# A decoder layer's conv norm: Newton product in the bank, later matmuls, longer VectorE estimates in the planner

## The chip, the cores and the metric

The kernel runs on one core of one Trainium2 chip. The metric is the time of the device for one execution in microseconds (us); the kernel is run several times and the median counts. The core has five engines with a queue each, worked off in order: TensorE (PE in the profile; PEld is its loading of weights), VectorE (DVE), ScalarE (ACT), GpSimd (POOL) and SyncE (SP), which issues the DMAs here. An engine waits at the head of its queue until what it needs is there, and everything behind that instruction waits with it.

## What is computed

One layer with two mixers side by side on 1024 positions of width 1024, in float32:

```python
def group_rms_norm(x, g, n_groups, eps=NORM_EPS):
    shp = x.shape
    xg = x.reshape(shp[:-1] + (n_groups, shp[-1] // n_groups)).astype(jnp.float32)
    y = xg * lax.rsqrt(jnp.mean(xg * xg, axis=-1, keepdims=True) + eps)
    return (y.reshape(shp) * g.astype(jnp.float32)).astype(x.dtype)

def hybrid_mixer(u, w_in, conv_w, conv_norm_g, ret_norm_g, w_out):
    z = u @ w_in
    ...
    y_conv = cb * causal_dwconv3(cc * ch, conv_w)
    y_conv = group_rms_norm(y_conv, conv_norm_g, CONV_GROUPS)
    ...
    y_ret = group_rms_norm(o, ret_norm_g, RET_HEADS) * jax.nn.silu(rg)
    return jnp.concatenate([y_conv, y_ret], axis=-1) @ w_out

h = h + hybrid_mixer(rms_norm(h, norm1_g), w_in, conv_w, conv_norm_g, ret_norm_g, w_out)
h = h + sq_relu_mlp(rms_norm(h, norm2_g), w_up, w_down)
return rms_norm(h, final_norm_g)
```

The part of interest is `y_conv`: 512 channels in 8 groups of 64, each group of each position divided by its root mean square.

## The kernel before

Everything lies transposed: channels on the 128 partitions, positions along the free axis in two halves of 512, so that a tile is 128 x 1024 and an instruction works on 128 x 512. A column tile of `z = u @ w_in` is 128 output channels. For each float32 product the two factors are split into a high part and a rest (`wh` and `wl` for weights, `uh` and `ul` or the two halves of `U` for the right-hand side), and three matmuls hi x hi, hi x lo and lo x hi stand for one; all are 128 x 128 by 128 x 512 into a bank of PSUM. The high part of a piece of weights is a cast on ScalarE, the rest (`wl<-r,wh`) a subtraction on VectorE or GpSimd (`split_piece`); both have four buffers.

The columns go by turns: retention's q and k first, then column tiles 0 to 3 and 20 whole (`whole`), then four pairs (4,5), (6,7), (8,9), (10,11) by `pair_in`, then 21 whole, and at the end 22 and 23. A pair is worked out with seven products of 12 matmuls in place of eight; it needs sums of weight blocks (`r<-r,r`, on GpSimd) and sums of the right-hand side (`xs`, `U`), and VectorE adds each product from its bank to the parts of the result (`z<-z,b`). The conv group i has the three tiles 3i (C), 3i+1 (h) and 3i+2 (B); tiles 20 to 23 are gates. What follows a tile are small programs written as generators: `conv_h` forms a = C * h * R2 and the three-tap convolution `cv` (ScalarE starts it, VectorE adds two taps: `cv<-z,sm,cv`), `conv_b` forms B * R * cv and asks for the norm, `gate` does SiLU, `split_y` splits y for the output product.

`norm` (from L468) serves one conv tile and half: ScalarE squares (`t`) and casts to the high part (`s<-t`), VectorE or GpSimd takes the rest (`s<-t,s`), two matmuls with a block matrix of ones, `blkr` (L483 and L484), add the squares over each group of 64 channels into a bank. Then ScalarE takes a reciprocal root `rt` and from it `less` = rt^2 / (2 x 64), and VectorE refines by one Newton step: `less` = (bank + 64 eps) * less, then in `done` (L712) y = y * (-g) * rt and y = (less - 1.5) * y. In the profile these three are `r<-b,r`, `z<-z,less_g,r` and `z<-r,z`.

The order in all queues is set when the program is built. A planner (`background`) keeps a clock for TensorE, `now`, moved on by 2.72 us for each product or quarter tile (`slot`), and a clock for each of the other three. A generator yields what it wants next: a tuple of engines (the planner gives it the one that would be done first, and goes on with the generator that is done first of all), a key that another one marks, or a number: the time that must have passed between its data being ready and `now` before its matmuls are put into TensorE's queue. A yield is thus a point at which another program's instruction may be put in between. `Engine.cost` is the estimate for one instruction: a fixed part and one per column; for VectorE, where no argument is in a bank, up to as much again while GpSimd's clock is ahead. The wrapper `Engine` records every instruction, so that the profile puts them all on L74. Weight pieces are split by `prepare` in a fixed order; there the choice between VectorE and GpSimd hangs on the two clocks, too.

Of the kernel before, what the change touches and what calls it, by code (L numbers as in the profile page):

```python
# [13 lines left out]
ALU = mybir.AluOpType  # L14
# [13 lines left out]
EPS = 1e-6  # L28
# [12 lines left out]
IN_END = [22, 23]  # L41
SLOT, LOOK, PE_MARGIN, LATE = 2.72, 3.2, 1.2, 0.0
WARM = 10
NORM_MARGIN, STEP_MARGIN = 4.0, 0.3
UP_ORDER, MLP_ORDER = (1, 2, 5, 6, 3, 7, 4), (1, 2, 6, 5, 3, 7, 4)


class Engine:
# [7 lines left out]
    def cost(self, n, op="", bank=False):  # L56
        per_column = 6.3 if op == "reciprocal" else self.per_column
        cost = self.fixed + 1e-3 * n * per_column
        if self.beside and not bank and op != "reciprocal":
            begin = max(self.clock[self], self.now[0])  # L60
            cost += min(cost, max(0.0, 0.6 * (self.clock[self.beside] - begin)))
        return cost

    def __getattr__(self, op):
# [15 lines left out]
def hybrid_layer(  # L80
# [21 lines left out]
    dve = Engine(nc.vector, 0.13, 1.04, now, clock, pool)  # L102
# [17 lines left out]
    def nm(s):  # L120
        n_[0] += 1
        return f"{s}{n_[0]}"
# [6 lines left out]
    def tmp():  # L129
        return temps[-1].tile([P, H], F32, tag="t", name=nm("t"))  # L130

    def bank(pool_=None):
        return (pool_ or pm).tile([P, H], F32, tag="b", name=nm("b"))

    def f32(ap):
        return ap.bitcast(F32)
# [106 lines left out]
    b = bank(pr)  # L243
# [181 lines left out]
    def mark(key, eng):  # L425
        got[key] = clock[eng]
# [44 lines left out]
    def norm(y, w, inv_n, done):  # L471

        sq = tmp()
        sh = xp.tile([P, H], F32R, tag="s", name=nm("s"), bufs=4)
        yield (act,)
        act.square(sq, y)
        act.copy(sh, sq)
        eng = yield (dve, pool)
        slo = xp.tile([P, H], F32R, tag="s", name=nm("s"), bufs=4)
        eng.tensor_sub(slo, sq, f32(sh))  # L480
        yield NORM_MARGIN
        b = bank(pr)
        nc.tensor.matmul(b, w, sh, start=True, stop=False)  # L483
        nc.tensor.matmul(b, w, slo, start=False, stop=True)  # L484
        now[0] += 0.43
        yield (act,)
        rt = xp.tile([P, H], F32, tag="s", name=nm("r"), bufs=4)
        less = xp.tile([P, H], F32, tag="s", name=nm("r"), bufs=4)
        act.activation(rt, b, AF.Abs_reciprocal_sqrt, bias=eps, scale=inv_n)
        act.activation(less, rt, AF.Square, scale=(0.5 * inv_n) ** 0.5)  # L490
        yield (dve,)

        dve.scalar_tensor_tensor(less, b, EPS / inv_n, less, ALU.add, ALU.mult)
        yield from done(rt, less)
        parts_of_s[0] -= 2

    def norms():
        while asked and parts_of_s[0] <= 2:
            parts_of_s[0] += 2
            y, w, inv_n, done, ready, late = asked.pop(0)  # L500
            spawn(norm(y, w, inv_n, done), ready, late)
# [200 lines left out]
    def conv_b(i, half, z, out, psum):  # L702
        sl = hs[half]
        o = out[:, sl]
        eng = dve if psum else (yield (pool, dve))
        eng.tensor_mul(o, z, R[:, sl])
        yield "cv", i, half
        eng = yield (pool, dve)
        eng.tensor_mul(o, o, cvs[i][:, sl])
        y[i] = out  # L710

        def done(rt, less):  # L712
            yield (dve,)
            dve.scalar_tensor_tensor(o, o, less_g[:, i : i + 1], rt, ALU.mult, ALU.mult)
            dve.scalar_tensor_tensor(o, less, 1.5, o, ALU.subtract, ALU.mult)
            mark(("y", i, half), dve)

        asked.append((o, blkr, 1.0 / 64, done, clock[eng], LATE * half))
# [531 lines left out]
    for at, (n, p) in enumerate((n, p) for n in MLP_ORDER for p in range(EARLY)):  # L1250
        b = early[p].product(n)
# [311 lines left out]
```

## Time and profile before

| | |
|---|---|
| median of 3 runs | 1080.27 us (1080.08 to 1080.79) |
| the profiled execution | 1081.81 us |
| its span, first to last instruction | 1079.0 us |
| granted TensorE clock, mean | 0.997 |
| PE busy | 1060.5 us (98%) |
| DVE busy | 878.7 us (81%) |
| POOL busy | 538.0 us (50%) |
| ACT busy | 460.2 us (43%) |

The profile is of one execution. A busy TensorE is not one at its full rate: matmuls overlap, and the starts of two that follow each other tell more than their durations. In the rows, `out<-in` gives the tiles by name, without their numbers; "idle before" is the time in which the engine stood still just before, and the arrow names what ended that.

### The profile page before, as it was taken

How to read it: one execution, taken by the hardware profiler on the slowest of the kernel's cores; microseconds unless marked ns; L12 is line 12 of the kernel's file. 1: busy time of each engine (PE TensorE's matmuls, PEld its weight loads, DVE VectorE, ACT ScalarE, POOL GpSimd, SP SyncE). 2: the span in 40 equal slices, each digit the busy share in tenths (PEclk: the TensorE clock that was granted, in tenths of full speed). 3: DMA queues.
4: the chain of work that ended last, by engine and by line, in shares of the span. 5: the costliest groups of instructions: out<-in, count | busy, mean ns of one | idle time of the engine just before them, and what ended most of it. 6: DMA issues, size and time to landing. Idle time of an engine off the chain costs nothing.

```text
span 1079.0 us, 13854 instructions
## 1 busy us (share of the span) xinstructions
PE 1060.5 (98%) x4860; PEld 881.6 (82%) x4860; DVE 878.7 (81%) x1246; ACT 460.2 (43%) x904; POOL 538.0 (50%) x366
## 2 busy tenths in 40 slices
PE   9999999999989999999999999999999999999997
PEld 7888888887768888788788888888888888888886
DVE  7446546799998656699999989989899899899955
ACT  8211445663435544444433443433343344334453
POOL 6234223255753223559538358267276185384552
PEclk9999999999999999999999999999999999999999
DMA  7111122222223635050121211201301301200204
GB/s 274 62 59 39 40 70 78 75 79 73 78 59 118 215 104 188 1 195 21 48 88 39 69 49 49 79 30 57 90 21 50 98 20 50 88 20 20 69 30 156
DMA packets 39685, 82.25 MB, mean 76 GB/s; under 512 B 4544, under 2 KB 5696, under 8 KB 39616
## 3 DMA queue, kind: packets, MB, share of 16 engines
q1 hardware_dynamic: 39328, 80.85, 23.0%
q8 instruction: 38, 0.62, 0.2%
q10 hardware_dynamic: 288, 0.52, 0.1%
q14 instruction: 31, 0.25, 0.1%
HBM read 71.92 MB, written 9.44 MB: 75 GB/s over the span
## 4 chain that ended last, share of the span: by engine, by line
PE 79%; DVE 10%; POOL 4%; issue 3%; ACT 2%; DMA 1%; DVEq 0%; SPq 0%; POOLq 0%; ACTq 0%
PE b L403 46%; PE b L1276 22%; PE b L357 4%; PE b L1385 4%; DVE wl L74 2%; DVE z L74 2%; POOL z L74 1%; POOL r L74 1%; DVE t L74 1%; DVE x L74 1%; DVE U L74 1%; DVE q L74 1%; DVE xs L74 1%; ACT h L74 1%; DVE m L74 1%
## 5 line engine op out<-in xcount | busy, mean ns | idle before, releaser
L403 PE MATMUL b<-U,wh 128*128 128x512 f32 x1024 | 315.8, 390 | 1.8 <-DVE x L74 1.1
L74 ACT CAST wh<-r 128x512 fp32r<-128x512 f32 x286 | 175.9, 620 | 321.2 <-PE b L403 134.5
L74 DVE TENSOR_TENSOR wl<-r,wh 128x512 fp32r<-128x512 f32 x251 | 231.8, 926 | 91.4 <-ACT wh L74 90.5
L74 POOL TENSOR_TENSOR r<-r,r 128x512 f32<-128x512 f32 x136 | 209.9, 1546 | 116.3 <-DVE wl L74 65.6
L1276 PE MATMUL b<-V,wh 128*128 128x512 f32 x784 | 242.0, 389 | 0.5 <-POOL V L74 0.4
L403 PEld LDWEIGHTS b<-U,wh 128*128 128x128 f32 x1024 | 191.8, 188 | 42.6 <-issue 1.9
L74 DVE TENSOR_TENSOR x<-x,b 128x512 f32<-128x512 f32 (+1 forms) x312 | 195.6, 673 | 30.2 <-PE b L1385 14.2
L403 PE MATMUL b<-U,wl 128*128 128x512 f32 x512 | 199.5, 390 | 0.3 <-POOL wl L74 0.3
L1276 PEld LDWEIGHTS b<-V,wh 128*128 128x128 f32 x784 | 147.1, 188 | 32.3 <-POOL V L74 0.8
L74 POOL TENSOR_TENSOR t<-t,t 128x512 f32<-128x512 f32 x70 | 106.4, 1524 | 97.9 <-ACT t L74 51.9
L1276 PE MATMUL b<-V,wl 128*128 128x512 f32 x392 | 152.5, 389 | 0.0
L74 POOL TENSOR_TENSOR wl<-r,wh 128x512 fp32r<-128x512 f32 x35 | 48.6, 1394 | 160.7 <-ACT wh L74 153.5
L403 PEld LDWEIGHTS b<-U,wl 128*128 128x128 f32 x512 | 96.2, 188 | 21.2 <-POOL wl L74 0.7
L403 PE MATMUL b<-uh,wh 128*128 128x512 f32 x304 | 103.4, 399 | 2.3 <-DVE z L74 2.3
L403 PE MATMUL b<-uh,wl 128*128 128x512 f32 x304 | 100.8, 391 | 1.1 <-DVE wl L74 1.1
L403 PE MATMUL b<-ul,wh 128*128 128x512 f32 x304 | 101.0, 392 | 0.0
L1276 PEld LDWEIGHTS b<-V,wl 128*128 128x128 f32 x392 | 73.5, 188 | 15.2
L74 POOL TENSOR_TENSOR V<-t,V 128x512 fp32r<-128x512 f32 x35 | 49.6, 1416 | 67.3 <-ACT V L74 67.3
L74 DVE TENSOR_TENSOR t<-t,b 128x512 f32<-128x512 f32 x112 | 75.8, 677 | 1.7 <-POOL t L74 1.2
L74 ACT ACTIVATE t<-t 128x512 f32<-128x512 f32 x64 | 40.2, 631 | 79.8 <-DVE t L74 79.2
L74 DVE TENSOR_TENSOR V<-t,V 128x512 fp32r<-128x512 f32 x63 | 70.3, 1116 | 0.0
L403 PEld LDWEIGHTS b<-uh,wl 128*128 128x128 f32 x304 | 57.3, 189 | 13.9 <-DVE wl L74 1.5
(178 smaller groups left out, 1422.1 us busy)
## 6 DMA issues: line engine op xcount, KB each, us to landing
r<-w_up_t SPq DMA_DIRECT2D x64, 256.0 KB, 2.6
r<-w_down_t SPq DMA_DIRECT2D x56, 256.0 KB, 2.7
r<-w_in_t SPq DMA_DIRECT2D x48, 256.0 KB, 2.7
xt<-xT SPq DMA_DIRECT2D x16, 256.0 KB, 5.4
xs<-xT SPq DMA_DIRECT2D x8, 512.0 KB, 4.9
r<-w_out_t SPq DMA_DIRECT2D x16, 256.0 KB, 2.7
x<-xT SPq DMA_DIRECT2D x8, 512.0 KB, 8.9
k<-x SPq DMA_DIRECT2D x6, 512.0 KB, 3.2
```

Of the source, the lines that this page charges most:

```text
L74: return f(out, *args, **kw)
L357: nc.tensor.matmul(vb[i], a[k][:, i * P : (i + 1) * P], b[k // 2][:, vs], start=(k == 0 and a is uh and b is vh), stop=(k == KT - 1 and a ...
L403: nc.tensor.matmul(b, a[:, k, :], rhs(n, k)[r], start=(start and i == 0), stop=(stop and i == len(ops) - 1),)
L1276: nc.tensor.matmul(b, a, r, start=(i == 0), stop=(i == len(ops) - 1))
L1385: nc.tensor.matmul(z, a, b, start=(k == 0 and t == 0), stop=(k == 3 and t == 2))
```

## The change

Three things are changed, and the planner then puts many instructions elsewhere.

- The planner: the wait in front of a norm's matmuls is 6.5 us in place of 4.0, and VectorE's estimate is lengthened as if GpSimd's clock stood 1.0 us later than it does.
- The first Newton product writes its result into the bank of the sums in place of the tile `less`. The last product reads it there, so that it has one input in PSUM and one in SBUF.
- A yield stands between the last two products.

```diff
-NORM_MARGIN, STEP_MARGIN = 4.0, 0.3
+NORM_MARGIN, STEP_MARGIN, POOL_LATE = 6.5, 0.3, 1.0
...
-            cost += min(cost, max(0.0, 0.6 * (self.clock[self.beside] - begin)))
+            cost += min(cost, max(0.0, 0.6 * (self.clock[self.beside] + POOL_LATE - begin)))
...
-        dve.scalar_tensor_tensor(less, b, EPS / inv_n, less, ALU.add, ALU.mult)
-        yield from done(rt, less)
+        dve.scalar_tensor_tensor(b, b, EPS / inv_n, less, ALU.add, ALU.mult)
+        yield from done(rt, b)
...
         def done(rt, less):
             yield (dve,)
             dve.scalar_tensor_tensor(o, o, less_g[:, i : i + 1], rt, ALU.mult, ALU.mult)
+            yield (dve,)
             dve.scalar_tensor_tensor(o, less, 1.5, o, ALU.subtract, ALU.mult)
             mark(("y", i, half), dve)
```

The number of instructions on TensorE is the same. VectorE's queue has 1170 rows where it had 1185, GpSimd's 384 where it had 370; in the stretch of the norms VectorE gives four net and GpSimd takes six more. Of the two orders below the numbers behind a name count tiles in the order of their making, so they differ from one program to the other; what tells the places apart are the names in front.

First piece: TensorE's queue, where before the norm of conv tile 2, first half, stood at the end of pair (8,9) (bank b_2683) and ahead of pair (10,11) (b_2717). Before:

```order
L403 MATMUL b_2683<-U_2224,wh_2602 128x512 x2
L403 MATMUL b_2683<-U_2224,wl_2603 128x512
L483 MATMUL b_2703<-s_2612,blkr 128x512
L484 MATMUL b_2703<-s_2634,blkr 128x512
L403 MATMUL b_2717<-uh_157,wh_2626 128x512
L403 MATMUL b_2717<-ul_165,wh_2626 128x512
```

Now the norm's bank is b_2747, and it stands behind the second product of pair (10,11), b_2727, ahead of the third, b_2758:

```order
L403 MATMUL b_2727<-uh_164,wh_2645 128x512
L403 MATMUL b_2727<-ul_172,wh_2645 128x512
L403 MATMUL b_2727<-uh_164,wl_2646 128x512
L483 MATMUL b_2747<-s_2631,blkr 128x512
L484 MATMUL b_2747<-s_2655,blkr 128x512
L403 MATMUL b_2758<-U_1566,wh_2670 128x512 x2
```

The norm's two matmuls moved by two products, 24 matmuls. The six norms of conv tiles 1 to 3 move by 12, 24, 24, 24, 12 and 24; the two of conv tile 0 by 12 each.

Second piece: VectorE's queue towards the end of pair (10,11): a norm's Newton products and the adding of products, down to the bank that column tile 21 takes over next (b_2813 before, b_2803 now). Before:

```order
L74 SCALAR_TENSOR_TENSOR cv_2759<-z_2536,sm,cv_2759 128x511
L74 SCALAR_TENSOR_TENSOR cv_2759<-z_2536,sm,cv_2759 128x510
L74 SCALAR_TENSOR_TENSOR r_2784<-b_2780,r_2784 128x512
L74 SCALAR_TENSOR_TENSOR z_2535<-z_2535,less_g,r_2783 128x512
L74 SCALAR_TENSOR_TENSOR z_2535<-r_2784,z_2535 128x512
L74 TENSOR_TENSOR z_2716<-z_2716,b_2792 128x512
L74 TENSOR_TENSOR z_2715<-z_2716,b_2761 128x512
L74 TENSOR_TENSOR z_2715<-z_2715,b_2813 128x512
```

Now:

```order
L74 SCALAR_TENSOR_TENSOR b_2747<-b_2747,r_2751 128x512
L74 SCALAR_TENSOR_TENSOR z_2535<-z_2535,less_g,r_2750 128x512
L74 TENSOR_TENSOR wl_2772<-r_2606,wh_2771 128x512
L74 SCALAR_TENSOR_TENSOR z_2535<-b_2747,z_2535 128x512
L74 SCALAR_TENSOR_TENSOR cv_2777<-z_2536,sm,cv_2777 128x511
L74 SCALAR_TENSOR_TENSOR cv_2777<-z_2536,sm,cv_2777 128x510
L74 TENSOR_TENSOR z_2702<-z_2702,b_2782 128x512
L74 TENSOR_TENSOR z_2701<-z_2702,b_2758 128x512
L74 TENSOR_TENSOR z_2701<-z_2701,b_2803 128x512
```

What stands ahead of the last three is the first half's Newton step where it was the second half's, with a low half of weights between its last two products. Further up, in pair (6,7), the low half of the fifth product stood behind two `cv` products (cv_2250 twice, then wl_2376) and now stands ahead of them (wl_2373, then cv_2269 twice).

Third piece: GpSimd's queue in pair (8,9): the sums of weight blocks for pair (10,11) (`r`), B * R of conv tile 2 (z_2535 with R) and low halves. Before:

```order
L74 TENSOR_TENSOR wl_2650<-r_2554,wh_2649 128x512
L74 TENSOR_TENSOR r_2578<-r_2578,r_2606 128x512
L74 TENSOR_TENSOR r_2529<-r_2578,r_2529 128x512
L74 TENSOR_TENSOR r_2554<-r_2554,r_2529 128x512
L74 TENSOR_TENSOR r_2578<-r_2606,r_2529 128x512
L74 TENSOR_TENSOR s_2710<-t_2659,s_2660 128x512
L74 TENSOR_TENSOR wl_2731<-r_2554,wh_2730 128x512
```

Now:

```order
L74 TENSOR_TENSOR z_2535<-z_2535,cv_2559 128x512
L74 TENSOR_TENSOR r_2579<-r_2579,r_2606 128x512
L74 TENSOR_TENSOR r_2522<-r_2579,r_2522 128x512
L74 TENSOR_TENSOR r_2554<-r_2554,r_2522 128x512
L74 TENSOR_TENSOR r_2579<-r_2606,r_2522 128x512
L74 TENSOR_TENSOR z_2535<-z_2535,R 128x512
L74 TENSOR_TENSOR wl_2717<-r_2554,wh_2716 128x512
```

A product with `cv`, which VectorE did before, now stands ahead of the four sums, and one with `R` ahead of the low half; a norm's rest (`s_2710`) has gone to VectorE.

## The prediction

> **What bounds the kernel now.** I read the table of stages first, then the waits of TensorE, then its timeline at each wait, and last the groups of VectorE and GpSimd in the same stretch. The table of stages (busy time and count of each engine, granted clock, DMA) shows a stretch in which TensorE runs without a break and the 100 us in which the conv norms are worked off:
>
> ```profile
> 360.00:380.00 20.00, 20.00 (x90) 16.58 (x89) 12.52 (x18) 10.10 (x18) 2.97 (x2) 1.00 0.72 255
> 240.00:340.00 100.00, 94.55 (x400) 75.35 (x399) 91.62 (x105) 44.00 (x73) 53.88 (x36) 0.98 0.28 90
> ```
>
> TensorE does 90 matmuls in 20 us where nothing holds it, and 400 in the 100 us from 240 to 340, 40 to 50 fewer than at that rate. VectorE is busy for 91.6 of those 100 us: here it is the engine that others wait for. Elsewhere the kernel is a nearly unbroken row of matmuls that the change leaves as they are. TensorE's own waits between 234 and 340 us (what ended them: total, times, longest):
>
> ```profile
> PE b L403 <- DVE z L74: 2.3, 1, 2.3
> PE b L403 <- DVE wl L74: 1.1, 1, 1.1
> PE b L483 <- ACT s L74: 1.0, 1, 1.0
> ```
>
> The ends of matmuls are modelled, so I price each wait from start to start in TensorE's timeline (start, duration, line, count, idle time before):
>
> ```profile
> 265.52 0.39 PE L403 MATMUL b<-ul,wh 128*128 128x512 f32 x1
> 267.03 0.50 PE L403 MATMUL b<-uh,wl 128*128 128x512 f32 x1 [1.12 <-DVE wl L74]
> 267.37 0.40 PE L403 MATMUL b<-uh,wh 128*128 128x512 f32 x1
> ...
> 269.70 0.47 PE L484 MATMUL b<-s,blkr 128*128 128x512 f32 x1
> 270.13 0.51 PE L483 MATMUL b<-s,blkr 128*128 128x512 f32 x1
> 270.86 0.50 PE L484 MATMUL b<-s,blkr 128*128 128x512 f32 x1 [0.22 <-DVE s L74]
> 271.20 0.62 PE L403 MATMUL b<-U,wh 128*128 128x512 f32 x2
> ...
> 295.80 0.40 PE L403 MATMUL b<-U,wl 128*128 128x512 f32 x1
> 297.17 0.50 PE L483 MATMUL b<-s,blkr 128*128 128x512 f32 x1 [0.97 <-ACT s L74]
> 297.89 0.50 PE L484 MATMUL b<-s,blkr 128*128 128x512 f32 x1 [0.23 <-DVE s L74]
> 298.23 0.40 PE L403 MATMUL b<-uh,wh 128*128 128x512 f32 x1
> ...
> 306.41 0.39 PE L483 MATMUL b<-s,blkr 128*128 128x512 f32 x1
> 307.13 0.50 PE L484 MATMUL b<-s,blkr 128*128 128x512 f32 x1 [0.33 <-DVE r L74]
> 307.46 0.62 PE L403 MATMUL b<-U,wh 128*128 128x512 f32 x2
> ...
> 317.68 0.62 PE L403 MATMUL b<-U,wh 128*128 128x512 f32 x2
> 318.14 0.39 PE L403 MATMUL b<-U,wl 128*128 128x512 f32 x1
> 318.36 0.39 PE L403 MATMUL b<-uh,wh 128*128 128x512 f32 x1
> 321.06 0.79 PE L403 MATMUL b<-uh,wh 128*128 128x512 f32 x1 [2.31 <-DVE z L74]
> ...
> 324.74 0.62 PE L403 MATMUL b<-uh,wl 128*128 128x512 f32 x2
> ```
>
> From 317.68 to 318.36 three matmuls start in 0.68 us, 0.227 each; what a step takes beyond that is lost. Four terms come out. **N**, the norms' own matmuls, whose input is not ready: 0.20 + 0.50 + 0.11 after 269.70, 1.14 + 0.49 + 0.11 after 295.80, 0.49 + 0.10 after 306.41, together 3.1 us. **W**, a weight piece's low half late at 267: 1.28 + 0.11 = 1.4 us. **B**, a bank that VectorE has not emptied at 321: 2.70 − 0.23 = 2.5 us. **C**, slow matmuls behind B: the nine that start from 321.06 to 324.74 take 3.68 us where 2.04 would do, 1.6 us. The sum is 8.6 us, and nothing in this stretch can bring more than that but for small change.
>
> **The change: the norms' matmuls.** The wait in front of them goes from 4.0 to 6.5 us of the planner's time, and its slot is 2.72, so they move by one product or two. The first piece of order shows one that stands 24 matmuls later, 5.4 us at 0.227; the two at 269 move by 12 and 24, the one at 306 by 24. None of the waits in N was over 1.8 us, so inputs that are ready when they were would no longer be waited for: N is worth up to 3.1. Behind a late norm wait its Newton products on VectorE and then y; the last y is needed by the output products, 72 matmuls (16 us) behind the last norm now, so I cost that delay at nothing; without that cover it would be up to 5.4. In the same place ScalarE gets two more table loads, since a gate now falls between the last two norms:
>
> ```profile
> 336.63 1.28 ACT L74 ACT_TABLE_LOAD x1
> ```
>
> 2 × 1.28 = 2.6 us under the same 16 us: nothing.
>
> **The change: VectorE and GpSimd.** What each instruction costs there, first the groups between 234 and 334 us (count, busy, mean ns), then all between 215 and 340 us (ns: least, median, most), and three in a row:
>
> ```profile
> L74 DVE TENSOR_TENSOR wl<-r,wh 128x512 fp32r<-128x512 f32 x17 | 19.7, 1158 | 3.2 <-ACT wh L74 3.0
> L74 DVE SCALAR_TENSOR_TENSOR z<-r,z 128x512 f32<-128x512 f32 x5 | 6.4, 1277 | 0.2
> L74 POOL TENSOR_TENSOR r<-r,r 128x512 f32<-128x512 f32 x12 | 17.9, 1496 | 4.0 <-DMA r<-w_in_t 2.3 <-DVE wl L74 1.3
> ```
> ```profile
> L74 DVE TENSOR_TENSOR wl<-r,wh x18: 675/692/1783, 221.7 to 333.8; 128x512 fp32r<-128x512 f32 x18
> L74 DVE SCALAR_TENSOR_TENSOR r<-b,r x8: 676/679/683, 228.7 to 337.6; 128x512 f32<-128x512 f32 x8
> L74 DVE SCALAR_TENSOR_TENSOR z<-r,z x8: 691/1177/1672, 230.5 to 339.0; 128x512 f32<-128x512 f32 x8
> ```
> ```profile
> 305.84 0.67 DVE L74 TENSOR_TENSOR z<-z,b 128x512 f32<-128x512 f32 x1
> 306.44 0.68 DVE L74 SCALAR_TENSOR_TENSOR r<-b,r 128x512 f32<-128x512 f32 x1
> 307.04 1.82 DVE L74 SCALAR_TENSOR_TENSOR z<-z,less_g,r 128x512 f32<-128x512 f32 x1
> ```
>
> An instruction with one input in a bank takes 0.68 always; one with both in SBUF takes 0.69 or anything up to 1.8. The difference is GpSimd: VectorE's 105 instructions at the step of 0.60 that the last three rows show would be 63 us, it was busy for 91.6, and the excess of 28.6 over GpSimd's 36 instructions is 0.8 us for each. One that GpSimd does costs it 1.50.
>
> Newton's last product now reads the bank, and a weight piece may go between the last two (second piece of order). From the evacuation of column tile 20 to the bank of B, VectorE has 80 instructions before and 75 now: 49 with both inputs in SBUF become 41 (four last products that now read a bank, four net that went elsewhere), 31 with a bank become 34. GpSimd has 33 in that part before, 39 now. The account at mean prices: four products from 1.28 to 0.68 save 2.4, four moved ones at 1.16 save 4.6, one more of 0.68 gone makes 7.7 us off VectorE; six more on GpSimd put back 0.8 each, 4.8. Net 2.9 us. The ends: 7.7 if none of the six meets VectorE, and with the removed ones at their price alone (0.69) 3.4 − 6 × 1.1 = −3.2, where 1.1 is 1.78 − 0.68.
>
> VectorE paces TensorE here, so this account and not the list of waits sets the sum. Up to the bank TensorE was 7.0 us behind an unbroken run (N 3.1, W 1.4, B 2.5). 7.0 − 2.9 leaves 4.1, wherever it is waited for. C: waits of 1.1 and 1.0 us brought no slow matmuls, the one of 2.3 did; if what is left comes in pieces, C goes, if at the bank at once, it stays. I take half, 0.8. **Sum: 2.9 + 0.8 = 3.7 us.** The profiled execution took 1081.81, 2.8 more than its span of 1079.0; 1081.81 − 3.7 = 1078.1. The median of the runs is 1.54 under the profiled one, so 1076.6.
>
> Three more edits I cost at nothing. Ahead of that part six instructions (three low halves, two products for the right-hand sides, one of a norm) go from VectorE to GpSimd, where each takes 0.8 longer (1.50 against 0.69); both have room there,
>
> ```profile
> 120.00:240.00 120.00, 119.03 (x656) 102.20 (x655) 83.82 (x171) 67.20 (x207) 45.42 (x32) 1.00 0.20 71
> ```
>
> with GpSimd busy for 45 of 120 us; without it the price is 4.8. A result written into a bank has no row (only TensorE writes banks here); the nearest is r<-b,r, which reads one in 0.68 against 0.69 from SBUF, so 0, with ends of −0.01 and +1.1 each, as if it were always held; the upper one, 8 × 1.1 = 8.8, lies beyond the third rival below and has its share of that chance. The Trainium skill (Perfetto Trace Analysis, Optimizing Scalar/DVE Operations) gives VectorE about 125 ns of access overhead on PSUM against 60 on SBUF, which would speak against this edit; by it the sixteen products of eight norms would lose 16 × 0.065 = 1.0 us by estimate, and the sum would be 2.7. The rows of 0.68 and 0.69 do not show that difference. And the norm's bank is held for the two instructions longer that stand between (second piece of order), some 2 us; its pool of four has at least two products, 5.4 us, to go before it comes round. Without that cover it is 2 us each.
>
> **The rivals.** *Only the queue's order was wrong* (chance 0.18): the late halves and norms were there for the taking, and VectorE's work fits once nothing is queued badly. For it: the wl of 267 stood behind two cv products in VectorE's queue and now stands ahead of them. Against: 91.6 busy of 100. All four terms go: 1080.27 − 8.6 = 1071.7.
>
> *GpSimd gives back what it takes* (0.20): the six more instructions each hold VectorE for the full 1.1, and 7.7 − 6.6 = 1.1 us is left (1079.2), or they hold it for 0.8 and what was removed had stood free, 3.4 − 4.8 = 1.4 us lost (1081.7); likeliest between, 1080.4. For it: medians of 0.69 against maxima of 1.78. The Trainium skill says the same in that section: moving work between VectorE and GpSimd may not help, since they share a read port.
>
> *GpSimd becomes the bound* (0.12, the other side). The third piece of order shows its queue. The z<-z,cv in it waits for VectorE's cv and holds four r, for which ScalarE's casts wait, and a wl that TensorE needs. Six more at 1.50 are 9.0 us; GpSimd was idle for 46 of the 100 us, mostly waiting in order. If its idle time takes in less than half of the 9.0, more is added than the 4.5 of N and W that this wait replaces, and the stage is longer than before; if none, 1080.27 + 9.0 − 4.5 = 1084.8.
>
> That the change does nothing is excluded by the order.
>
> **How the numbers follow.** The forecast has 0.50, with 1073.3 to 1078.1 as its own range (VectorE's account between 7.0 and 2.2 saved). A measurement of this kernel can tell about 0.2%, 2.2 us, from no change. Faster: 0.50 + 0.18 = 0.68; within: 0.20; slower: 0.12. The range from 1071.5 to 1081.5 takes in the first two rivals and leaves out the third.
>
> **What would show it.** Right: no wait at L483 or L484, z<-b,z at 0.68 in all eight, VectorE still at about 90% between 240 and 340, and TensorE's loss there at 4 to 6 us, most of it for banks or wl. Wrong: wl or cast waits on GpSimd at the head of TensorE's list (third rival), VectorE's both-in-SBUF rows at 1.5 and more in the mean (second), or a stretch of 90 matmuls in every 20 us (first). A b<-b,r above 0.7 would undo the price of the bank.

## The result, and the profile after

The changed kernel took 1070.55 us (median of 4 runs, 1070.03 to 1071.17), the kernel before 1080.17 beside it (1077.12 to 1080.79). The two medians differ by 9.6 us; the ratio over all runs is 0.992 with a 95% interval of 0.9907 to 0.9933: 8.6 us less, 7.2 to 10.0, and this is the gain used below. The forecast was 3.7 us less, 1076.6. The measured times lie below its range, which began at 1071.5; 8.6 us off the 1080.27 from which it was worked out would be 1071.7, at the very edge of it. So the direction was right and the size under half.

The table of stages of the changed kernel, from 240 to 340 us (busy time and count of PE, PEld, DVE, ACT and POOL, granted clock, DMA):

```profile
240.00:340.00 100.00, 100.00 (x443) 82.78 (x442) 91.22 (x103) 48.19 (x76) 68.45 (x45) 1.00 0.28 87
```

TensorE does 443 matmuls where it did 400: 43 at 0.227 us are 9.8 us. VectorE is as busy as before (91.2 against 91.6) and GpSimd busier (68.5 against 53.9). Among TensorE's waits between 234 and 340 us the profile lists none. The norms' matmuls at 269 now stand among others at the full pace, and the wait B is gone, as TensorE's and VectorE's timeline show:

```profile
268.58 0.39 PE L403 MATMUL b<-U,wl 128*128 128x512 f32 x1
268.81 0.39 PE L483 MATMUL b<-s,blkr 128*128 128x512 f32 x1
269.04 0.39 PE L484 MATMUL b<-s,blkr 128*128 128x512 f32 x1
269.26 0.62 PE L403 MATMUL b<-U,wh 128*128 128x512 f32 x2
...
309.07 2.19 DVE L74 TENSOR_TENSOR z<-z,b 128x512 f32<-128x512 f32 x3
311.20 0.39 PE L403 MATMUL b<-U,wl 128*128 128x512 f32 x1
311.43 0.62 PE L403 MATMUL b<-uh,wh 128*128 128x512 f32 x2
```

The second of the two `uh,wh` matmuls writes the bank of B. It starts at 311.43 + 0.227 = 311.66, and VectorE emptied that bank at 309.07 + 2.19 = 311.26: 0.4 us to spare. The groups between 234 and 334 us (count, busy, mean ns, idle before), then all of the norm's two products between 215 and 345 us (ns: least, median, most):

```profile
L74 DVE TENSOR_TENSOR wl<-r,wh 128x512 fp32r<-128x512 f32 x19 | 22.6, 1188 | 3.0 <-ACT wh L74 2.7
L74 DVE SCALAR_TENSOR_TENSOR z<-b,z 128x512 f32<-128x512 f32 x7 | 4.8, 681 | 0.1
```
```profile
L74 DVE SCALAR_TENSOR_TENSOR b<-b,r x8: 684/690/700, 226.5 to 334.8; 128x512 f32<-128x512 f32 x8
L74 DVE SCALAR_TENSOR_TENSOR z<-b,z x8: 676/679/691, 233.7 to 336.6; 128x512 f32<-128x512 f32 x8
```

The last product is 0.68 in all eight (691 to 1672 ns before), and a result written into a bank takes 0.69 where one written into SBUF took 0.68. VectorE's low halves are hardly longer than before (1188 ns against 1158), although GpSimd does 45 instructions from 240 to 340 us and not 36.

**Where VectorE gained.** The execution profiled of before began more slowly. The same matmul of TensorE's, first in before and then in after:

```profile
204.75 0.71 PE L403 MATMUL b<-uh,wh 128*128 128x512 f32 x2
```
```profile
201.97 0.71 PE L403 MATMUL b<-uh,wh 128*128 128x512 f32 x2
```

So 2.8 us are taken off the times of before when its places are compared, and the other kernels below are shifted by the same matmul. Behind it the change first costs TensorE time. In the retention it waits twice for ScalarE's `h`, where before had no wait; the second of the two places, in before and then in after:

```profile
211.73 0.52 PE L663 MATMUL b<-ident,h 128*128 128x128 f32 x2
```
```profile
210.32 0.58 PE L663 MATMUL b<-ident,h 128*128 128x128 f32 x2 [0.35 <-ACT h L74]
```

That is 209.0 and 210.3 on one scale: 1.4 us lost. All six profiles of kernels with estimates longer by 1.0 show three waits at this line from 195 us on (1.7 to 1.8 us together), all six without the lengthening show one of 0.6 to 0.7. VectorE's timeline of before, at the evacuation of tile 20 (`z<-b,R`) and at the bank of B, then of after at tile 20:

```profile
240.90 1.28 DVE L74 TENSOR_TENSOR z<-b,R 128x512 f32<-128x512 f32 x2
...
319.53 1.48 DVE L74 TENSOR_TENSOR z<-z,b 128x512 f32<-128x512 f32 x2
```
```profile
235.48 1.27 DVE L74 TENSOR_TENSOR z<-b,R 128x512 f32<-128x512 f32 x2
```

From tile 20 to the bank of B: 240.90 to 321.01 before (80.1 us), 235.48 to 311.26 after (75.8), so 4.3 are gained. And VectorE comes to tile 20 at 238.1 before, once 2.8 are taken off, and 235.5 after: 2.65 ahead. Together 7.0 us at the bank of B, which is as much as N + W + B.

### The profile page after: what moved, and what is told of

Its sections match the earlier page's. It is cut to its first block, busy times and chain, and to the rows that moved or that the text cites. A ratio compares the mean times of both kernels' runs of the same rounds, so it can differ in the third digit from the quotient of the medians.

```text
span 1068.1 us, 13853 instructions
## 1 busy us (share of the span) xinstructions
PE 1054.8 (99%) x4860; PEld 879.2 (82%) x4860; DVE 870.8 (82%) x1231; ACT 463.6 (43%) x906; POOL 561.6 (53%) x381
## 4 chain that ended last, share of the span: by engine, by line
PE 90%; DVE 6%; ACT 2%; issue 1%; POOL 1%; DVEq 0%; ACTq 0%; POOLq 0%
PE b L403 55%; PE b L1277 23%; PE b L357 4%; PE b L1386 4%; DVE t L74 1%; DVE wl L74 1%; DVE x L74 1%; DVE m L74 1%; ACT h L74 1%; DVE q L74 1%; DVE V L74 1%; PE b L339 0%; PE b L595 0%; PE b L1436 0%; PE b L246 0%
## 5 line engine op out<-in xcount | busy, mean ns | idle before, releaser
L74 POOL TENSOR_TENSOR wl<-r,wh 128x512 fp32r<-128x512 f32 x36 | 51.4, 1432 | 119.3 <-ACT wh L74 116.5
L74 DVE TENSOR_TENSOR t<-t,b 128x512 f32<-128x512 f32 x112 | 75.8, 677 | 1.7 <-POOL t L74 1.2
```

The lines of the kernel that those rows point to most:

```text
L74: return f(out, *args, **kw)
```

## The experiments

Three theories stood against each other. **Theory 1**, the forecast's mechanism with a larger gain: VectorE paces TensorE; every us that VectorE comes earlier to the bank of B is won until no wait is left, and every us later is lost. **Theory 2**, the first rival: only the order of the queues was wrong; VectorE's idle time between tile 20 and the bank of B takes in small changes. (The expectations put it at 5.4 us; the two stretches less VectorE's busy time there give 5.2 in before and 6.1 in after.) **Theory 3**, the second and third rivals: GpSimd gives back what it takes, or is the bound. The kernel before ran on the same chip as each set of kernels (1079.35, 1078.87 and 1079.27 us in the three sets), so kernels are compared by their ratio to it. Where two are set against each other below, 0.001 is 1.08 us.

### Order and operand apart

Two kernels, each with the order of one and the operand of the other. The first has the queues of after and the Newton product in SBUF; the second the queues of before and the product in the bank. So that the order stays, the last product's estimate is told what the other kernel's would be. The edits, against after and against before:

```diff
-        dve.scalar_tensor_tensor(b, b, EPS / inv_n, less, ALU.add, ALU.mult)
-        yield from done(rt, b)
+        dve.scalar_tensor_tensor(less, b, EPS / inv_n, less, ALU.add, ALU.mult)
+        yield from done(rt, less)
...
-            dve.scalar_tensor_tensor(o, less, 1.5, o, ALU.subtract, ALU.mult)
+            dve.scalar_tensor_tensor(o, less, 1.5, o, ALU.subtract, ALU.mult, as_bank=True)
```
```diff
-        dve.scalar_tensor_tensor(less, b, EPS / inv_n, less, ALU.add, ALU.mult)
-        yield from done(rt, less)
+        dve.scalar_tensor_tensor(b, b, EPS / inv_n, less, ALU.add, ALU.mult)
+        yield from done(rt, b)
...
-            dve.scalar_tensor_tensor(o, less, 1.5, o, ALU.subtract, ALU.mult)
+            dve.scalar_tensor_tensor(o, less, 1.5, o, ALU.subtract, ALU.mult, as_bank=False)
```

> The order of all queues as in the kernel after, row for row; only the Newton product goes back into an SBUF tile, so that the last product has two SBUF inputs again. Theory 1 (VectorE paces TensorE, and the kernel after has only about 0.4 us to spare at the bank of B): four last products before that bank cost 0.5 to 0.6 us more each, 2.0 to 2.4 together; 1.6 to 2.0 of it becomes a wait at 311 us, with slow matmuls behind it up to 1.6 more: 1072 to 1074. Theory 2 (only the order of the queues was wrong, VectorE's own idle time takes in such lengthening): 1070.6, within 0.5 of the kernel after, no wait of TensorE from 240 to 340.

> The order of all queues as in the kernel before, row for row; only the Newton product stays in the bank, so that the last product reads it there. Theory 1 (VectorE paces TensorE): VectorE is 2.0 to 2.4 us earlier at the bank of B, whose wait shrinks from 2.5 to under 0.5 or is shared with N and W, and the slow matmuls behind it go: 1076 to 1078. Theory 2 (only the order of the queues was wrong): the waits stand where they stood, 1079.5 to 1080.3.

Measured: 1074.16 us, ratio 0.9951 (0.9939 to 0.9964), and 1075.32 us, 0.996 (0.9946 to 0.9974). Theory 1 had said 1072 to 1074 and 1076 to 1078, and misses both by less than 1 us. TensorE's waits between 234 and 345 us (total, times, longest), of the order of after with the product in SBUF, then of the order of before with it in the bank:

```profile
PE b L404 <- DVE z L75: 1.4, 1, 1.4
```
```profile
PE b L404 <- DVE z L75: 1.3, 1, 1.3
PE b L404 <- DVE wl L75: 0.6, 1, 0.6
PE b L485 <- POOL s L75: 0.3, 1, 0.3
PE b L485 <- DVE s L75: 0.2, 1, 0.2
```

The same instructions in the same queues, with nothing changed but where the last product's input lies: in the order of after the bank of B is late by 1.4 us, in the order of before the waits shrink. Theory 2 has no room for either. The order alone brings 4.9 thousandths (5.3 us), the operand alone 4.0 (4.3 us), both 8.0 (8.6 us), each to about 1.4 thousandths. VectorE's places say the same (times shifted as above, so that the matmul of 203 us falls together):

| | VectorE at tile 20 | bank of B empty | between |
|---|---|---|---|
| before | 238.1 | 318.2 | 80.1 |
| order of before, product in the bank | 237.2 | 314.5 | 77.3 |
| order of after, product in SBUF | 235.5 | 313.1 | 77.7 |
| after | 235.5 | 311.3 | 75.8 |

Between the two places the operand is worth 2.8 and 1.9 us; the prediction's 2.4 for four last products lies between.

### One part each

The kernel before with one part of the change: the wait of 6.5 (`m_margin`), VectorE's longer estimates (`m_late`), the product in the bank with the yield (`m_bank`). Then the kernel after with the wait at 4.0 again, and with the estimates as they were. The edits are the lines of the change itself:

```diff
-NORM_MARGIN, STEP_MARGIN = 4.0, 0.3
+NORM_MARGIN, STEP_MARGIN = 6.5, 0.3
```
```diff
-NORM_MARGIN, STEP_MARGIN = 4.0, 0.3
+NORM_MARGIN, STEP_MARGIN, POOL_LATE = 4.0, 0.3, 1.0
```
```diff
-        dve.scalar_tensor_tensor(less, b, EPS / inv_n, less, ALU.add, ALU.mult)
-        yield from done(rt, less)
+        dve.scalar_tensor_tensor(b, b, EPS / inv_n, less, ALU.add, ALU.mult)
+        yield from done(rt, b)
...
+            yield (dve,)
```
```diff
-NORM_MARGIN, STEP_MARGIN, POOL_LATE = 6.5, 0.3, 1.0
+NORM_MARGIN, STEP_MARGIN, POOL_LATE = 4.0, 0.3, 1.0
```
```diff
-NORM_MARGIN, STEP_MARGIN, POOL_LATE = 6.5, 0.3, 1.0
+NORM_MARGIN, STEP_MARGIN, POOL_LATE = 6.5, 0.3, 0.0
```

> The kernel before with the wait in front of the norm's matmuls at 6.5 alone. Theory 1 (VectorE paces TensorE): the waits N go, and TensorE comes to W and B earlier by as much and waits there longer: 1079.5 to 1080.5. Theory 2 (only the order was wrong): N goes and nothing takes its place, 1080.2 - 3.1 = 1077.1.

> The kernel before with VectorE's longer estimates alone: 20 instructions of 1185 leave VectorE, 19 more are on GpSimd. Theory 1 (VectorE paces TensorE): 5 to 6 us less up to the bank of B, as the order of the kernel after brought with its product in SBUF, and the norm's early place costs 0.4 to 1.3: 1073.5 to 1075 where the kernel before takes 1079. Theory 2 (only the order was wrong, the norms' place first of all): N stays with 3.1 us of waits and the rest goes, 1077. Theory 3 (GpSimd gives back what it takes): 1079.

> The kernel before with the Newton product in the bank and the yield between the last two products alone; the planner, which knows the cheaper product, moves a few instructions. Theory 1 (VectorE paces TensorE; the operand is what counts): as the operand in the order of before, 0.996 of the kernel before, 1075 to 1076 where that takes 1079. Theory 2 (only the order was wrong): 1078.5 to 1079.

> The kernel after with the wait in front of the norm's matmuls at 4.0 again, so that they stand earlier in TensorE's queue. Theory 1 (VectorE paces TensorE; N came from VectorE's being late): with VectorE ahead by 7 us the norm's inputs are ready at the earlier place too: 1070.6 to 1071.2. Theory 2 (only the order was wrong): N comes back, 3.1 us of waits at L483 and L484: 1073.7.

> The kernel after with VectorE's estimates as before, so that about 14 instructions return from GpSimd to VectorE. Theory 1 (VectorE paces TensorE): what moved them had saved 2 to 5 us of VectorE up to the bank of B; they come back as waits at a bank or a low half there, wherever the norms stand: 1074 to 1077. Theory 2 (only the order was wrong): the norms stay late and N stays gone; W and B may return in part: 1071 to 1073.

| kernel | us | ratio to before | 95% interval |
|---|---|---|---|
| before, wait 6.5 alone | 1078.43 | 0.9996 | 0.9987 to 1.0004 |
| before, estimates alone | 1074.98 | 0.9963 | 0.995 to 0.9975 |
| before, bank and yield alone | 1074.53 | 0.9961 | 0.9948 to 0.9973 |
| after, wait 4.0 | 1072.01 | 0.9932 | 0.992 to 0.9945 |
| after, estimates as before | 1074.12 | 0.9949 | 0.9936 to 0.9961 |

The three parts alone bring 0.4, 3.7 and 3.9 thousandths; their sum is 8.0, and so is the whole, though the intervals, 0.9 to 1.3 to either side of each, let the sum be off by 2. Theory 1 had these three right to about 1 us: the wait of 6.5 alone came out 1.1 below its range (before itself took 1078.87 in that set), bank and yield alone 0.5 below, the estimates alone within. TensorE's waits, of before with the wait of 6.5 alone and then of before with the estimates alone:

```profile
PE b L403 <- DVE z L74: 2.9, 1, 2.9
PE b L403 <- DVE wl L74: 1.9, 2, 1.0
```
```profile
PE b L484 <- DVE s L74: 1.7, 1, 1.7
PE b L403 <- DVE z L74: 1.3, 1, 1.3
```

The first is the clearest case against theory 2. N's 3.1 us are gone from L483 and L484, and B went from 2.3 to 2.9, the low halves from 1.1 to 1.9: TensorE came earlier to an engine that was still late. In the profile some 1.8 us of N stay won at the bank of B (316.4 against 318.2), while the median shows 0.4 with an interval to 1.4; that rest isn't settled. In the second a norm is waited for with 1.7 us, since its place is early and VectorE has not its `s`. With all else of the change, the early place costs 1.3 us by the ratios (intervals overlap), and its profile shows one wait:

```profile
PE b L484 <- POOL s L74: 0.6, 1, 0.6
```

That is more than theory 1's 0.1 to 0.7, and far from theory 2's 3.1. Without the longer estimates the kernel after loses 3.1 us, at the bank and at a low half, as theory 1 had it:

```profile
PE b L403 <- DVE z L74: 1.7, 1, 1.7
PE b L403 <- DVE wl L74: 0.4, 1, 0.4
```

### Doses on VectorE

Extra products on VectorE ahead of the evacuation of tile 20, which write the same values over again and stand in no estimate: four and twelve in the kernel after, four in the kernel before.

```diff
+        if h == 0 and half == 0:
+            for _ in range(4):
+                nc.vector.tensor_mul(g[:, sl], z, R[:, sl])
         eng.tensor_mul(g[:, sl], z, R[:, sl])
```

> The kernel after with four more VectorE products from a bank (the same product over again, 0.68 us each and 0.60 apart) ahead of the evacuation of tile 20, which no estimate of the planner sees; the order is else the same. Theory 1 (VectorE paces TensorE, some 0.4 us to spare at the bank of B): VectorE comes 2.4 us later there and TensorE waits 2.0 at about 313, with up to 1.6 of slow matmuls behind it: 1072.5 to 1074.2. Theory 2 (order only; VectorE stands idle for 5.4 us in that stretch, which takes it in): 1070.6.

> As with four, but twelve: 7.2 us of VectorE. Theory 1: 6.8 us of waits in TensorE from 240 to 340, first at low halves and norms and then at banks, 1077.4 to 1079: the dose takes the kernel after back to the time of the one before. Theory 2: 7.2 less the idle 5.4, so 1072.4.

> The kernel before with the same four products at the same place. Theory 1 (nothing to spare there): all of it is lost, 1080.2 + 2.4 = 1082.6. Theory 2 (the idle time of VectorE, 8 of 100 us, takes it in): 1080.2 to 1081.

Measured: 1073.83 us, 0.9953 (0.9936 to 0.9969); 1079.31, 1.0006 (0.9996 to 1.0015); 1081.35, 1.002 (1.0006 to 1.0033). The doses were larger than meant, as VectorE's rows of the kernel with twelve show:

```profile
L726 DVE TENSOR_TENSOR z<-b,R x12: 678/691/692, 235.2 to 243.2; 128x512 f32<-128x512 f32 x12
```

Eleven steps in 8.0 us are 0.73 each, not 0.60: twelve put tile 20 off by 8.7 us (235.2 to 243.9), four by 2.9. The kernel after lost 3.6 us to four (0.9953 less 0.992) and 9.3 to twelve (1.0006 less 0.992; 1079.31 is a little over theory 1's 1077.4 to 1079), the kernel before 2.2 (0.6 to 3.6) to four. TensorE's waits in the kernel after with four, then with twelve:

```profile
PE b L403 <- DVE z L74: 2.1, 1, 2.1
PE b L403 <- DVE wl L74: 0.2, 1, 0.2
```
```profile
PE b L403 <- ACT wh L74: 2.7, 1, 2.7
PE b L403 <- DVE z L74: 2.1, 1, 2.1
PE b L403 <- DVE wl L74: 0.6, 2, 0.4
```

Within these intervals a us put on VectorE is a us of the kernel, on either side of the change, and 8.7 us of it take the kernel after back to the time of the kernel before. VectorE's idle time took in none of it: with the twelve the bank of B is empty 8.8 us later than in the kernel after (320.1 against 311.3), with the four 3.1. Theory 2 gave 0 for four and 1.8 for twelve.

### More onto GpSimd

The kernel after with VectorE's estimates lengthened as if GpSimd stood 2.0 us later, and 6.0.

```diff
-NORM_MARGIN, STEP_MARGIN, POOL_LATE = 6.5, 0.3, 1.0
+NORM_MARGIN, STEP_MARGIN, POOL_LATE = 6.5, 0.3, 2.0
```

> The kernel after with VectorE's estimates as if GpSimd were 2.0 us later in place of 1.0: 11 fewer on VectorE, 10 more on GpSimd. Theory 1 (VectorE paced; the kernel after has no wait left from 240 to 340): within 0.7 of the kernel after, which is 1070.3 where the kernel before takes 1079; what VectorE gains is not waited for. Theory 3 (GpSimd becomes the bound): 10 instructions of 1.5 us, of which GpSimd's idle time takes half: low halves or casts late on GpSimd, 1073 to 1078.

> The same with 6.0 us: 23 fewer on VectorE than in the kernel after, 24 more on GpSimd, 36 us there. Theory 1: VectorE has spare time, but GpSimd, 68 of 100 us busy from 240 to 340 in the kernel after, comes over 90 there and is waited for: 1073 to 1080. Theory 3 (GpSimd the bound from fewer on): over 1080. If neither, VectorE's lead is all that counts: within 0.7 of the kernel after.

Measured: 1082.04 us, 1.0028 (1.0015 to 1.004), and 1083.07, 1.0041 (1.0028 to 1.0055): 11.7 us slower than the kernel after with 2.0, slower than the kernel before. Both theories' numbers for 2.0 missed on the low side; for 6.0 theory 3 had it right (over 1080), though GpSimd was busy there for 81 of the 100 us and not over 90, as theory 1 had it. VectorE's lead was no longer what counted. In the kernel with 2.0, TensorE's waits between 195 and 260 us, and GpSimd's timeline at the second:

```profile
PE b L663 <- ACT h L74: 5.1, 2, 3.7
PE b L403 <- POOL U L74: 3.0, 1, 3.0
```
```profile
240.06 1.29 POOL L74 TENSOR_TENSOR wl<-r,wh 128x512 fp32r<-128x512 f32 x1 [4.69 <-ACT wh L74]
241.31 1.30 POOL L74 TENSOR_TENSOR xs<-xs 128x512 f32<-128x512 f32 x1
242.69 3.32 POOL L74 TENSOR_TENSOR xs<-xs,xs 128x512 f32<-128x512 f32 x2
246.09 1.59 POOL L74 TENSOR_TENSOR xs<-xs 128x512 f32<-128x512 f32 x1
247.64 1.71 POOL L74 TENSOR_TENSOR U<-xs,U 128x512 fp32r<-128x512 f32 x1
```

GpSimd stands 4.7 us in front of a low half whose cast is not there, with four sums and a `U` behind it, and TensorE needs that `U`: the third rival's mechanism, a wait in GpSimd's order with work behind it that others need. GpSimd was busy for 76 of the 100 us from 240 to 340, not 100; it is late by its order, not by being full. The other wait, 3.7 us at 215, is for ScalarE's `h` in the retention. It needs small sums (`m`) from VectorE, which in this order stand behind a low half, which waits for its cast, and two evacuations:

```profile
210.17 1.37 DVE L74 TENSOR_TENSOR wl<-r,wh 128x512 fp32r<-128x512 f32 x1 [0.60 <-ACT wh L74]
211.46 1.27 DVE L74 TENSOR_TENSOR z<-b,R 128x512 f32<-128x512 f32 x2
212.66 0.84 DVE L74 SCALAR_TENSOR_TENSOR m<-m,bq 128x2 f32<-128x2 f32 x1
```

The retention is also where the kernel after loses its 1.4 us with 1.0. Both waits of the kernel with 2.0 were followed by matmuls at half the clock. So the gain lies between 0.0 (3.1 us short of it) and 2.0 (11.7 us short); of the values tried 1.0 is the best, and no version beat the kernel after.

## Why the prediction was right or wrong

**The bound** was right: VectorE paced TensorE from tile 20 to the bank of B. The doses show it on both sides of the change.

**N, W and B** were right as a list of what could be won: 7.0 us, and 7.0 us is what VectorE gained at the bank of B. All of it went, not 2.9 of it. The forecast had the bound and the waits right and mis-sized what VectorE would gain, in the two steps that follow.

**"Ahead of that part six instructions go from VectorE to GpSimd ... both have room there"** is the first step that failed: what lies ahead of tile 20 was costed at nothing, and VectorE comes out of it 2.65 us earlier. The row it leaned on was a mean over 120 us (VectorE busy for 83.8 of them). The last 20 us ahead of tile 20, in the kernel before:

```profile
222.00:242.00 20.00, 20.00 (x90) 16.57 (x89) 19.76 (x20) 11.42 (x18) 12.58 (x8) 1.00 0.00 1
```

VectorE had no room there: it was already 19.8 of 20 us busy, TensorE at 90 matmuls in 20 us did not yet wait, and a lead won here counts at the bank of B. But the six moved instructions do not explain the 2.65. The kernel with the longer estimates alone takes these and two more off VectorE ahead of tile 20, and its VectorE gets there at 238.2 (shifted), no sooner than before: what it saves goes into the retention, where VectorE falls 1.4 us behind. With the wait of 6.5 alone it gets there at 236.4, with bank and yield alone at 235.8. What the rows show is products of the norms that changed sides. In before two stand ahead of tile 20 (evacuated at 240.90), in after they stand behind it (235.48):

```profile
237.88 1.77 DVE L74 SCALAR_TENSOR_TENSOR z<-z,less_g,r 128x512 f32<-128x512 f32 x1
239.69 0.69 DVE L74 SCALAR_TENSOR_TENSOR z<-r,z 128x512 f32<-128x512 f32 x1
```
```profile
236.67 1.24 DVE L74 SCALAR_TENSOR_TENSOR z<-z,less_g,r 128x512 f32<-128x512 f32 x1
239.78 0.68 DVE L74 SCALAR_TENSOR_TENSOR z<-b,z 128x512 f32<-128x512 f32 x1
```

They took 2.4 us of VectorE (237.88 to 240.30). So tile 20 is one place in the program, but not in VectorE's order, and an account that begins there leaves out what went across. It should have begun where VectorE last stood still. How the 2.65 divides is not shown.

**"Six more on GpSimd put back 0.8 each, 4.8"** was too much. The 7.7 us off VectorE shrank to 4.3 and not to 2.9, so 3.4 came back. Between tile 20 and the bank of B VectorE is busy for 74.95 us of 80.1 before and for 69.72 of 75.8 after: 5.2 less, of which 0.9 went into longer idle time. For the 100 us by the prediction's own reckoning: 103 instructions at 0.60 are 61.8, busy 91.2, an excess of 29.4 over 45 of GpSimd's, where it was 28.6 over 36. With nine more of GpSimd's VectorE's excess grew by 0.8 us in all. A mean price of 0.8 was taken for the price of one more. That VectorE had fewer instructions left with both inputs in SBUF (49 became 41) fits this; it was not tried apart.

**C, "if at the bank at once, it stays"**, does not follow from the length of the wait. The kernel before with four doses waits there as long, 2.32 us, and the kernel with the wait of 6.5 longer, 2.86; the clock stays whole in both. Granted clock (third number from the end) from 322 to 324 us: before, before with four doses, before with the wait of 6.5:

```profile
322.00:324.00 2.00, 2.00 (x6) 1.53 (x5) 1.21 (x2) 1.50 (x3) 0.20 (x1) 0.50 0.00 0
```
```profile
322.00:324.00 2.00, 2.00 (x11) 1.65 (x10) 1.18 (x2) 1.75 (x3) 0.66 (x1) 1.00 0.00 0
```
```profile
322.00:324.00 2.00, 2.00 (x10) 1.67 (x9) 1.93 (x2) 0.08 (x1) 2.00 (x2) 1.00 0.00 0
```

It hangs on how the wait falls on steps of the clock that begin elsewhere in each execution (last section). The two profiled spans differ by 10.9 us, 8.1 without the slow start of before: the 9.8 of the 43 matmuls, less the 1.4 lost in the retention and small change. 1.6 of the 8.1 are C's, and the 6.5 without it lie under the measured 7.2 to 10.0. So some executions behind the median of before probably had slow matmuls too; how many isn't recorded.

**The bank's price**, 0, was right: 0.684 to 0.700 for the write, 0.676 to 0.691 for the last product. VectorE's extra cost on PSUM, which the Trainium skill gives (Perfetto Trace Analysis, Optimizing Scalar/DVE Operations: about 125 ns against 60 on SBUF), would have been 1.0 us by estimate. The rows differ by 0.01 and contradict it for these instructions.

**The norms' matmuls** wait no more, as foretold, and y behind them is not waited for. But "worth up to 3.1" holds only together with the rest: alone the edit brought 0.4.

**The rivals.** "Only the queue's order was wrong" gave 1071.7, the nearest number, for a reason that fell: order and operand each bring about half, and VectorE has nothing to spare. That its 8.6 us equal the measured 8.6 is luck: they hold C, which hangs on the execution, and leave out the 1.4 lost in the retention. "GpSimd gives back what it takes" fell with the 0.8 us. "GpSimd becomes the bound" did not happen at this size, and did at twice the lengthening.

## What to carry to other kernels

When an engine paces another, find where it last stood still and count its work from there: a lead won ahead of the first visible wait counts too, work can change sides of any place chosen later, and a mean busy share over a long stretch hides where the engine is already full. List the waits, then ask of each edit whether it makes the late engine earlier or only moves the wait; an edit that only lets the waiting engine come sooner (the norms' later place alone) is paid back at the next wait. Work moved to a neighbouring engine's queue costs little until it stands behind a wait with something urgent after it, and then much: try the next step of such a constant on both sides, and look for its first small waits elsewhere in the program.

## What was not expected of the hardware

The granted clock falls after some waits of TensorE and not after others of like length: after 2.31 (before), 2.70 (after with twelve doses), 2.98 and 3.66 us (estimates by 2.0) it was 0.50, after 2.14, 2.32 and 2.86 it stayed at 1.00. In the kernel with twelve doses, behind the wait of 2.70:

```profile
248.00:250.00 2.00, 1.82 (x5) 1.42 (x5) 2.00 (x4) 0.90 (x2) 1.39 (x1) 0.50 0.29 72
```

The traces' record of the clock shows what tells them apart. Each change of the clock lies a whole number of steps of 3.413 us behind the start of the full clock: in before it is full from 10.34 us, 0.50 from 320.95 (91 steps) to 324.36 (92); with twelve doses it is 0.50 for one step, with estimates by 2.0 twice for two, by 6.0 once for two. In the step just ahead of each of these stretches TensorE stood still for 2.2 to 3.4 us (2.20 in before, from 317.54 to 320.95). Where the clock stayed full, no step held more than 1.7: the wait of 2.32 fell on two steps with 1.1 and 1.2, that of 2.86 with 1.3 and 1.6. So a wait of 2.3 to 2.9 us costs its length alone or 1.6 us and more on top of it, by where it falls, and the steps begin elsewhere in each execution (4.6 to 10.3 us after its start). The Trainium skill (TensorE: Matmul & The Clock Gate, HAM oscillation) warns of gaps over about 3.4 us. Here shorter ones brought the half clock too. Its remark (What's actually happening) that the window of activity runs freely agrees with these steps.

Products that write one tile over and over stood 0.73 us apart, where products into different tiles stand 0.60 apart. Why was not tried.
